# HGRN2 decay levels on 64 keys by 64 queries in place of 128 by 128

## The chip, the cores and the metric

The kernel runs on one core of one Trainium2 chip. The metric is device time in microseconds (us) of one execution; the median of several executions is compared. The profile is taken by the hardware profiler during one more execution of the same program, and all views of the trace below come from that one. Engines are named as the profile names them: PE is TensorE's matmul, PEld its weight load, DVE is VectorE, ACT is ScalarE, POOL is GpSimd, SP is SyncE.

## The reference

Two layers of a trunk over 640 tokens (512 latent tokens and 128 context tokens, width 1024). Each layer normalises and modulates its input, projects it once, mixes tokens in three ways (a Fourier transform, six heads of retention, six heads of HGRN2), projects back, and runs a SwiGLU feed-forward network. The part that the change touches is HGRN2, per head with 64 key and 64 value channels:

```python
rel = bc[:, :, :, None, :] - bc[:, :, None, :, :]
dec = jnp.exp(jnp.where(tri[:, :, None], rel, -jnp.inf))
A = jnp.sum(qc[:, :, :, None, :] * kc[:, :, None, :, :] * dec, axis=-1)
o = inter + jnp.einsum('bhij,bhjv->bhiv', A, vc)
```

Here bc is the running sum of the logarithm of the forget gate. Each pair of a query i and a key j is weighted, channel by channel, by the product of the gates between them. The scan runs once forward and once backward, and the two outputs are added. The reference uses chunks of 64 tokens; the kernel uses chunks of 128 and gets the same sums.

## The kernel before

**Stages.** A short start normalises the input and makes the first modulation. Then each layer has a stage of mixers (`mixers`, `hgrn`, `retention`, `fourier`) and a feed-forward stage (`feed`). The mixers of layer 0 lie between about 90 and 340 us of the trace, those of layer 1 between about 960 and 1170 us. Most of PE's time in both stages goes to products in which each operand is split into a high and a low part (lines 219 to 221, three products for one), whose weights ACT and DVE split on the fly (lines 206 and 207).

**HGRN2 by levels.** `hgrn(l, ct)` handles two heads at once: head 0 lies on partitions 0 to 63, head 1 on partitions 64 to 127. It runs four times in a layer: for ct = 0, 1 and 2 over the 512 latent tokens (nu = 4 chunks of 128) and once for the context tokens (nu = 3: its one chunk for each of the three pairs of heads). The scores of a chunk, transposed with keys on partitions and queries in columns, are built in AT. First a product without decay gives the diagonal (pd, line 809). Then seven levels follow, s = 1, 2, 4, ..., 64. At a level the chunk is cut into blocks of s tokens, and the two blocks of each neighbouring pair are queries and keys of each other. The product pl (line 824) is made over the whole chunk, all 128 keys by all 128 queries, though at level `lev` only the entries whose blocks are neighbours are wanted. For levels 0 to 4 these are picked by a copy under a mask (line 843, COPY_PREDICATED on DVE); for levels 5 and 6 ACT copies the wanted rectangles (line 847).

**Order within a level.** POOL multiplies the keys K by decays (line 832) and the table of decays Tm (line 835). ACT gathers the keys of the next level into C (line 799). DVE multiplies half of the queries Qx by decays (line 839); it can do so only when pl has read them, and the next pl waits for it. So the loop through PE is: pl of a level, Qx on DVE, pl of the next.

**Order of the work.** PE's order is written by the program: `Order` keeps a planned clock that `o.pe(us)` moves on, and generators such as `hgrn` give control back with `yield us` so that other units of work (projections of 2.6 or 3.9 us, parts of retention and of the Fourier transform) come in between. After each pl the clock is moved on by 0.44 * nu, and each level ends with `yield P["lev"]`, 2.4. The instructions of the other engines are put in order by a scheduler when the program is built. In layer 0 a further thread (`modulation`, lines 312 and 314) puts the remaining modulation on DVE, with loads from DRAM.

After the levels the keys are transposed (KT, line 867), states are built (U, line 697), and `cross_out` makes the output from S, Qx and AT (lines 737 and 741).

Of the kernel before, what the change touches and what calls it, by code (L numbers as in the profile page):

```python
# [11 lines left out]
U8 = mybir.dt.uint8  # L12
# [17 lines left out]
def pick(t2, p0, p1, off, dims):  # L30
    b = t2[p0:p1, 0:1]
    return bass.AP(b.tensor, b.offset + off, [list(list(b.ap)[0])] + [list(d) for d in dims])
# [119 lines left out]
class Kernel:  # L152
# [312 lines left out]
    def mixers(self, l, hT, mp):  # L465
        nc, a, o = self.nc, self.a, self.o
# [6 lines left out]
        self.raws, self.mix = [None] * 6, [None] * NK  # L473
        mskf = self.m4("mskf", (128, 7, 128))
        nc.sync.dma_start(mskf, a["masks"])
        self.msk = mp.tile([128, 7, 128], U8, name="msk")
        nc.vector.tensor_copy(self.msk, mskf)
        self.free(mskf)
        self.forget_bounds(l)
        self.PF, self.PK = self.m3("PF", (128, 2, 3, 128)), self.m3("PK", (128, 2, 3, 128))  # L480
# [285 lines left out]
    def hgrn(self, l, ct):  # L766

        nc = self.nc  # L770
        prev = {0: None, 1: 0, 2: 1, None: 2}[ct]
        need = [("B", 2 if ct is None else ct)] + ([("Hlast", prev)] if ct != 0 else [])
        yield lambda: self.have(*need) and self.can(m4=4, m2=3)
        self.mark(("H", ct))
        if ct is None:
            bases = (self.PF, self.PK, self.Pq)
            F, K = (t.rearrange("p d c w -> p d (c w)") for t in (self.PF, self.PK))
            q = self.Pq.rearrange("p c w -> p (c w)")
        else:
            bases = self.hg.pop(ct)  # L780
            F, K, q = bases
        nu = 3 if ct is None else 4
        W = nu * 128
        Qx = self.m4("Qx", (128, 2, W))
        ks = self.m2("ks", (128, W))
        nc.gpsimd.tensor_tensor(ks, K[:, 0, :], K[:, 1, :], ALU.add)
        nc.vector.tensor_tensor(Qx, F, q.unsqueeze(1).to_broadcast([128, 2, W]), ALU.mult)
        AT = self.m4("AT", (128, 2, nu, 128))
        Qf, Kf = Qx.rearrange("p d w -> p (d w)"), K.rearrange("p d w -> p (d w)")
        Tt, toff = F.rearrange("p d w -> p (d w)"), 0  # L790
        Tn, tnext = self.m4("Tm", (128, 2 * W)), 0

        Cs = deque(self.m2("C") for _ in range(2))

        def composite(lev):
            s = 1 << lev
            C = self.mem.again(Cs.popleft(), "C", (128, W))
            Cs.append(C)
            nc.scalar.copy(pick(C, 0, 128, 0, [[2 * s, W // s // 2], [s, 2], [1, s]]),
                           pick(Kf, 0, 128, 0, [[2 * s, W // s // 2], [W + s, 2], [1, s]]))  # L800
            return C

        C = composite(0)
        yield 2.0
        pd = [self.ps("pd") for _ in range(2)]
        for u in range(nu):
            for hh in range(2):
                pr, us = slice(64 * hh, 64 * hh + 64), slice(u * 128, (u + 1) * 128)
                nc.tensor.matmul(pd[hh][:, us], ks[pr, us], q[pr, us], start=True, stop=True)
        self.o.pe(0.44 * nu)  # L810
        self.free(ks, bases[2])
        for hh in range(2):
            nc.scalar.copy(AT[:, hh], pd[hh][:, 0:W].rearrange("p (u i) -> p u i", u=nu))
        yield 1.0
        S = None
        for lev in range(7):
            s = 1 << lev
            nb = W // s
            np_ = nb // 2
            pl = [self.ps("pl") for _ in range(2)]  # L820
            for u in range(nu):
                for hh in range(2):
                    p0 = 64 * hh
                    nc.tensor.matmul(pl[hh][:, u * 128:(u + 1) * 128], C[p0:p0 + 64, u * 128:(u + 1) * 128],  # L824
                                     pick(Qf, p0, p0 + 64, u * 128, [[2 * s, 64 // s], [W + s, 2], [1, s]]),
                                     start=True, stop=True)
            self.o.pe(0.44 * nu)

            for d in range(2):
                kv = pick(Kf, 0, 128, d * (W + s), [[2 * s, np_], [1, s]])  # L830
                tv = pick(Tt, 0, 128, toff + (nb + 1 if d == 0 else 0), [[2, np_], [0, s]])
                self.kv.tensor_tensor(kv, kv, tv, ALU.mult)
            if lev < 6:
                C = composite(lev + 1)
            self.kv.tensor_tensor(pick(Tn, 0, 128, tnext, [[np_, 2], [1, np_]]),
                                  pick(Tt, 0, 128, toff, [[nb, 2], [2, np_]]),
                                  pick(Tt, 0, 128, toff + 1, [[nb, 2], [2, np_]]), ALU.mult)
            qv = pick(Qf, 0, 128, 0, [[W + s, 2], [2 * s, np_], [1, s]])
            nc.vector.tensor_tensor(qv, qv, pick(Tt, 0, 128, toff + 1, [[nb - 1, 2], [2, np_], [0, s]]), ALU.mult)
            for hh in range(2):  # L840
                pv = pl[hh][:, 0:W].rearrange("p (u i) -> p u i", u=nu)
                if lev < 5:
                    nc.vector.copy_predicated(AT[:, hh], self.msk[:, lev, :].unsqueeze(1).to_broadcast([128, nu, 128]), pv)
                else:
                    for b in range(128 // s):
                        rows, cols = (slice(s * i, s * i + s) for i in (b, b ^ 1))
                        nc.scalar.copy(AT[rows, hh, :, cols], pv[rows, :, cols])
            Tt, toff, tnext = Tn, tnext, tnext + 2 * np_
            if lev == 0:
                self.free(bases[0])  # L850
            if lev == 5:
                self.free(*Cs)
            if lev == 4 and ct is not None:
                yield lambda: self.can(m4=1)
                S = self.new_states(l, 1, ct)
            if lev == 1:
                self.mark(("Hfree", ct))
            yield P["lev"]
        self.mark(("Hlast", ct))
        yield lambda: self.can(m3=1)  # L860
        pk = [self.ps("pk") for _ in range(2)]
        KT = self.m3("KT", (128, 2, 3, 128))
        for d in range(2):
            for n in range(3):
                u = n if ct is None or d == 0 else n + 1
                nc.tensor.transpose(pk[d][:, n * 128:(n + 1) * 128], K[:, d, u * 128:(u + 1) * 128], self.ident)
            nc.scalar.copy(KT[:, d], pk[d][:, 0:384].rearrange("p (n c) -> p n c", n=3))
        self.o.pe(0.7)
        self.free(bases[1])
        yield 1.6  # L870
        Tsc = lambda d, c: Tn[:, toff + (1 - d) * nu + c:toff + (1 - d) * nu + c + 1]
        yield lambda: self.have(*(("V", l, g, t) for g in (0, 1) for t in range(5)))
        self.cross_states(l, 1, ct, KT, Tsc, self.VH, S)
        self.free(Tn)
        yield P["co"]
        yield lambda: ct is None or self.can(ax=1)
        self.cross_out(1, ct, AT, S, (Qx[:, 1, :], Qx[:, 0, :]), self.VH)
        self.free(Qx)
        if ct is None:
            self.mark(("Hdone",), 0.0)  # L880
# [608 lines left out]
```

## Time and profile before

| what | value |
|---|---|
| median of 3 runs | 1744.54 us (1740.31 to 1745.72) |
| profiled execution | 1746.83 us |
| its span from first to last instruction | 1745.1 us |
| mean granted TensorE clock | 0.990 |
| busy: PE, DVE, ACT, POOL | 1683.2, 1072.5, 694.9, 451.5 us |

Busy times of different engines overlap. A busy time of PE is the union of its matmuls, each from its start to its modelled end; matmuls are pipelined and overlap, so how fast they follow one another is read from the starts and from the length of a run of equal ones. A product of float32 operands leaves two records for each call in the program, one of float32r operands leaves one.

### The profile page before, as it was taken

The numbers are of one execution on the slowest core, as the hardware profiler recorded it, in microseconds if no ns is written. First come the engines' busy times: TensorE is split into PE (matmuls) and PEld (weight loads), VectorE is DVE, ScalarE is ACT, GpSimd is POOL, SyncE is SP. The second block draws the span as 40 slices with busy tenths as digits, with TensorE's granted clock in tenths as the row PEclk, the third lists the DMA queues.
The fourth block names the chain that finished last, engine by engine and source line by source line (L and its number), as shares of the span: only waits on it lengthen the run. The fifth ranks groups of instructions, "written<-read, shape, count | busy, mean of one in ns | idle before, by whom it ended". The sixth has DMA issues, their size and how long they took to land.

```text
span 1745.1 us, 29155 instructions
## 1 busy us (share of the span) xinstructions
PE 1683.2 (96%) x11634; PEld 1547.1 (89%) x11634; DVE 1072.5 (61%) x1851; ACT 694.9 (40%) x1362; POOL 451.5 (26%) x473
## 2 busy tenths in 40 slices
PE   6989989999999999999999999999999999999997
PEld 4878878898999999989989998879799999999996
DVE  4597996548668776877484556674654434343428
ACT  4633443745544443434164444367253122121210
POOL 2233432103255453644052233220230000000001
PEclk9999989999999999999999999999999999999999
DMA  8544521242356554544222121113234222222301
GB/s 328 165 129 128 159 63 40 83 169 85 117 190 203 162 181 131 181 135 152 73 101 93 61 74 60 40 59 103 103 109 157 73 73 73 73 85 61 96 26 61
DMA packets 71239, 194.42 MB, mean 111 GB/s; under 512 B 12208, under 2 KB 12992, under 8 KB 71104
## 3 DMA queue, kind: packets, MB, share of 16 engines
q1 hardware_dynamic: 66816, 182.10, 32.5%
q0 software_dynamic: 4000, 10.35, 1.8%
q8 instruction: 91, 1.49, 0.3%
q14 instruction: 44, 0.36, 0.1%
q10 hardware_dynamic: 288, 0.11, 0.0%
HBM read 186.47 MB, written 6.06 MB: 110 GB/s over the span
## 4 chain that ended last, share of the span: by engine, by line
PE 80%; DVE 7%; ACT 3%; issue 2%; POOL 2%; DMA 1%; SPq 0%; DVEq 0%; ACTq 0%; POOLq 0%
PE pg L221 6%; PE pu L221 6%; PE pu L220 6%; PE pu L219 6%; PE pg L220 6%; PE pg L219 6%; PE dps L221 5%; PE dps L220 5%; PE dps L219 5%; PE pl L824 2%; PE p L219 2%; PE ops L221 2%; PE ops L219 2%; PE ops L220 2%; PE p L220 2%
## 5 line engine op out<-in xcount | busy, mean ns | idle before, releaser
L207 DVE TENSOR_TENSOR wlo<-wraw,whi 128x1024 fp32r<-128x1024 f32 x204 | 266.1, 1307 | 255.8 <-ACT whi L206 253.6
L206 ACT CAST whi<-wraw 128x1024 fp32r<-128x1024 f32 x206 | 215.1, 1048 | 405.9 <-PE pg L220 126.2
L316 POOL TENSOR_TENSOR wm<-wm,csb 128x512 f32<-128x512 f32 x112 | 179.8, 1625 | 183.0 <-DVE jb L312 156.8
L221 PE MATMUL pg<-h2T,wlo 128*128 128x384 f32 (+1 forms) x704 | 218.2, 310 | 3.0 <-DVE wlo L207 3.0
L219 PE MATMUL pg<-h2T,whi 128*128 128x384 f32 (+1 forms) x704 | 218.4, 310 | 0.0
L220 PE MATMUL pg<-h2T,whi 128*128 128x384 f32 (+1 forms) x704 | 217.8, 309 | 0.0
L220 PE MATMUL pu<-h2T,whi 128*128 128x384 f32 (+1 forms) x704 | 217.2, 308 | 0.0
L219 PE MATMUL pu<-h2T,whi 128*128 128x384 f32 (+1 forms) x704 | 217.2, 308 | 0.0
L221 PE MATMUL pu<-h2T,wlo 128*128 128x384 f32 (+1 forms) x704 | 217.2, 308 | 0.0
L340 POOL TENSOR_SCALAR bnve<-bnag 128x1 f32<-128x1 f32 x40 | 13.9, 351 | 645.9 <-DVE bnag L338 636.6
L219 PE MATMUL dps<-whi,ah 128*128 128x512 f32 x440 | 171.5, 390 | 0.0
L221 PE MATMUL dps<-whi,al 128*128 128x512 f32 x440 | 171.5, 390 | 0.0
L220 PE MATMUL dps<-wlo,ah 128*128 128x512 f32 x440 | 171.4, 389 | 0.0
L312 DVE SCALAR_TENSOR_TENSOR jb<-wm,csb 128x512 bf16<-128x512 f32 x160 | 149.0, 931 | 14.2 <-DMA wm<-in_w_modT 8.4
L221 PEld LDWEIGHTS pg<-h2T,wlo 128*128 128x128 f32 x704 | 134.0, 190 | 3.5 <-DVE wlo L207 3.4
L219 PEld LDWEIGHTS pg<-h2T,whi 128*128 128x128 f32 x704 | 134.2, 191 | 0.3
L220 PEld LDWEIGHTS pg<-h2T,whi 128*128 128x128 f32 x704 | 134.2, 191 | 0.3
L289 ACT ACTIVATE wm<-wm 128x512 f32<-128x512 f32 x112 | 70.8, 632 | 158.1 <-POOL wm L316 157.8
L221 PEld LDWEIGHTS pu<-h2T,wlo 128*128 128x128 f32 x704 | 133.6, 190 | 0.0
L220 PEld LDWEIGHTS pu<-h2T,whi 128*128 128x128 f32 x704 | 133.6, 190 | 0.0
L219 PEld LDWEIGHTS pu<-h2T,whi 128*128 128x128 f32 x704 | 133.6, 190 | 0.0
L1194 DVE TENSOR_TENSOR sg<-sg,pu 128x256 f32<-128x256 f32 x88 | 42.7, 485 | 119.8 <-PE pu L221 112.9
(273 smaller groups left out, 3830.5 us busy)
## 6 DMA issues: line engine op xcount, KB each, us to landing
wm<-in_w_modT SPq DMA_DIRECT2D x160, 256.0 KB, 2.9
wraw<-in_w_gate SPq DMA_DIRECT2D x44, 512.0 KB, 3.7
wraw<-in_w_up SPq DMA_DIRECT2D x44, 512.0 KB, 3.6
wraw<-in_w_down SPq DMA_DIRECT2D x44, 512.0 KB, 3.6
wraw<-in_w_fm SPq DMA_DIRECT2D x42, 512.0 KB, 3.6
wm<-in_w_mod SPq DMA_DIRECT2D x16, 512.0 KB, 10.2
wraw<-in_w_tm SPq DMA_DIRECT2D x16, 512.0 KB, 3.5
wraw<-in_w_out SPq DMA_DIRECT2D x16, 512.0 KB, 3.7
```

What stands on the lines that cost most here:

```text
L206: self.nc.scalar.copy(hi, raw)
L207: (eng or self.nc.vector).tensor_tensor(lo, raw, hi.bitcast(F32), ALU.subtract)
L219: mm(out, lh, rh, start=first, stop=False)
L220: mm(out, lh, rl, start=False, stop=False)
L221: mm(out, ll, rh, start=False, stop=last)
L289: keep(nc.scalar.activation(out=t, in_=t, func=AF.Copy, accum_out=d))
L312: keep(nc.vector.scalar_tensor_tensor(self.jb, wt, 1.0, csb[0], ALU.mult, ALU.mult, accum_out=d[0]))
L316: nc.gpsimd.tensor_tensor(wt, wt, csb[1], ALU.mult)
L340: nc.gpsimd.tensor_scalar(ve, ag[:, 1:2], EPS, None, ALU.add)
L824: nc.tensor.matmul(pl[hh][:, u * 128:(u + 1) * 128], C[p0:p0 + 64, u * 128:(u + 1) * 128], pick(Qf, p0, p0 + 64, u * 128, [[2 * s, 64 // s ...
L1194: nc.vector.tensor_tensor(sg, sg, pu[:, :n], ALU.mult)
```

## The change

The level products are made for halves of a chunk. Keys 0 to 63 meet only queries 0 to 63, and keys 64 to 127 only queries 64 to 127; each such product has 64 channels, 64 keys and 64 queries, and takes one quarter of the array: the head gives the rows, the half of the keys gives the columns. Up to level 5 the wanted pairs lie inside a half. At level 6 (s = 64) each half's keys meet the other half's queries. So there are 16 calls for nu = 4 where there were 8, in the order head 0 with half 0, head 0 with half 1, head 1 with half 0, head 1 with half 1, and then the next chunk.

Results are gathered in 64 columns: pd and pl fill half a bank of PSUM, and while levels 0 to 5 run, AT holds its scores in columns 0 to 63 of each chunk. Copies from pd and the masked copies are over half as many columns, and the mask has 5 levels and 64 columns in place of 7 and 128. At level 6 one more ACT copy moves the scores of the keys 64 to 127 to columns 64 to 127; then the two copies for each head fill the off-diagonal quarters. What is charged to the planned clock and the yields are as before.

```diff
-        self.msk = mp.tile([128, 7, 128], U8, name="msk")
-        nc.vector.tensor_copy(self.msk, mskf)
+        self.msk = mp.tile([128, 5, 64], U8, name="msk")
+        for b in (slice(0, 64), slice(64, 128)):
+            nc.vector.tensor_copy(self.msk[b], mskf[b, 0:5, b])
...
-        pd = [self.ps("pd") for _ in range(2)]
-        for u in range(nu):
-            for hh in range(2):
-                pr, us = slice(64 * hh, 64 * hh + 64), slice(u * 128, (u + 1) * 128)
-                nc.tensor.matmul(pd[hh][:, us], ks[pr, us], q[pr, us], start=True, stop=True)
+        A = AT.rearrange("p h u i -> p (h u) i")
+
+        def halves(name):
+            return [self.ps(name)[:, 0:W // 2].rearrange("p (u i) -> p u i", u=nu) for _ in range(2)]
+
+        def blocks():
+            for u in range(nu):
+                for hh in range(2):
+                    for b in range(2):
+                        t0 = u * 128 + 64 * b
+                        yield slice(64 * hh, 64 * hh + 64), slice(64 * b, 64 * b + 64), hh, u, b, t0
+
+        pd = halves("pd")
+        for pr, rows, hh, u, b, t0 in blocks():
+            nc.tensor.matmul(pd[hh][rows, u], ks[pr, t0:t0 + 64], q[pr, t0:t0 + 64], start=True, stop=True)
         self.o.pe(0.44 * nu)
         self.free(ks, bases[2])
         for hh in range(2):
-            nc.scalar.copy(AT[:, hh], pd[hh][:, 0:W].rearrange("p (u i) -> p u i", u=nu))
+            nc.scalar.copy(AT[:, hh, :, 0:64], pd[hh])
...
-            pl = [self.ps("pl") for _ in range(2)]
-            for u in range(nu):
-                for hh in range(2):
-                    p0 = 64 * hh
-                    nc.tensor.matmul(pl[hh][:, u * 128:(u + 1) * 128], C[p0:p0 + 64, u * 128:(u + 1) * 128],
-                                     pick(Qf, p0, p0 + 64, u * 128, [[2 * s, 64 // s], [W + s, 2], [1, s]]),
-                                     start=True, stop=True)
+            pl = halves("pl")
+            for pr, rows, hh, u, b, t0 in blocks():
+                if lev < 6:
+                    qs = pick(Qf, pr.start, pr.stop, t0, [[2 * s, 32 // s], [W + s, 2], [1, s]])
+                else:
+                    qs = Qf[pr, (1 - b) * W + t0 + 64 - 128 * b:(1 - b) * W + t0 + 128 - 128 * b]
+                nc.tensor.matmul(pl[hh][rows, u], C[pr, t0:t0 + 64], qs, start=True, stop=True)
...
+            if lev == 6:
+                nc.scalar.copy(A[64:128, :, 64:128], A[64:128, :, 0:64])
             for hh in range(2):
-                pv = pl[hh][:, 0:W].rearrange("p (u i) -> p u i", u=nu)
                 if lev < 5:
-                    nc.vector.copy_predicated(AT[:, hh], self.msk[:, lev, :].unsqueeze(1).to_broadcast([128, nu, 128]), pv)
+                    nc.vector.copy_predicated(AT[:, hh, :, 0:64], self.msk[:, lev, :].unsqueeze(1).to_broadcast([128, nu, 64]),
+                                              pl[hh])
+                elif lev == 5:
+                    for b in range(4):
+                        rows, cols = slice(32 * b, 32 * b + 32), slice(32 - 32 * (b % 2), 64 - 32 * (b % 2))
+                        nc.scalar.copy(AT[rows, hh, :, cols], pl[hh][rows, :, cols])
                 else:
-                    for b in range(128 // s):
-                        rows, cols = (slice(s * i, s * i + s) for i in (b, b ^ 1))
-                        nc.scalar.copy(AT[rows, hh, :, cols], pv[rows, :, cols])
+                    for b in range(2):
+                        rows = slice(64 * b, 64 * b + 64)
+                        nc.scalar.copy(AT[rows, hh, :, 64 - 64 * b:128 - 64 * b], pl[hh][rows])
```

## Rows read from the trace of the kernel before

**Rows 1.** The page: busy us by engine, share of the span, instructions.
```profile
PE 1683.2 (96%) x11634; PEld 1547.1 (89%) x11634; DVE 1072.5 (61%) x1851; ACT 694.9 (40%) x1362; POOL 451.5 (26%) x473
```

**Rows 2.** The page: the chain that ended last, share of the span by engine.
```profile
PE 80%; DVE 7%; ACT 3%; issue 2%; POOL 2%; DMA 1%; SPq 0%; DVEq 0%; ACTq 0%; POOLq 0%
```

**Rows 3.** Windows of the mixers: busy us (records) by engine, clock, DMA share, GB/s.
```profile
90.00:270.00 180.00, 159.31 (x1363) 144.00 (x1364) 158.99 (x336) 69.97 (x164) 64.05 (x76) 0.95 0.39 118
960.00:1170.00 210.00, 206.36 (x1941) 183.74 (x1940) 128.18 (x235) 94.66 (x223) 69.15 (x92) 0.99 0.20 61
```

**Rows 4.** What PE waited for, 90 to 340 us: total, times, longest.
```profile
PE pl L824 <- DVE Qx L839: 17.9, 12, 3.5
PE pr L906 <- DVE rx L542: 3.7, 2, 2.7
```

**Rows 5.** What PE waited for, 960 to 1170 us.
```profile
PE pr L906 <- DVE rx L542: 2.1, 2, 1.8
PE pl L824 <- ACT K L512: 0.7, 1, 0.7
```

**Rows 6.** Instructions of lines 824 and 809: duration ns min/median/max, first and last start.
```profile
L824 PE MATMUL pl<-Qx,C x840: 272/272/580, 97.1 to 1155.7; 64*128 64x128 f32 x168
...
L809 PE MATMUL pd<-q,ks x96: 272/272/373, 92.9 to 1070.0; 64*128 64x128 f32 x96
```

**Rows 7.** PE by time: pl of level 2, and its first records alone (start, length).
```profile
107.88 1.16 PE L824 MATMUL pl<-Qx,C 64*128 64x128 f32 x16 [0.20 <-DVE Qx L839]
...
107.88 0.60 PE L824 MATMUL pl<-Qx,C 64*128 64x128 f32 x6 [0.20 <-DVE Qx L839]
```

**Rows 8.** PE by time: pl of level 2 for nu = 3.
```profile
279.70 0.94 PE L824 MATMUL pl<-Qx,C 64*128 64x128 f32 x12
```

**Rows 9.** PE by time: pl of level 0 and of level 1.
```profile
97.07 1.57 PE L824 MATMUL pl<-Qx,C 64*128 64x128 f32 x16
...
103.39 1.23 PE L824 MATMUL pl<-Qx,C 64*128 64x128 f32 x16 [1.68 <-DVE Qx L839]
```

**Rows 10.** PE by time: U, products with 64 columns, whole and first records alone.
```profile
144.59 0.92 PE L697 MATMUL U<-VH,KT 128*64 128x64 f32 x24
...
144.59 0.63 PE L697 MATMUL U<-VH,KT 128*64 128x64 f32 x14
```

**Rows 11.** PE by time: the first modulation, four products side by side.
```profile
46.85 0.64 PE L248 MATMUL modps<-wm,cs 128*32 128x128 f32 x16
...
49.19 0.86 PE L248 MATMUL modps<-wm,cs 128*32 128x128 f32 x24
```

**Rows 12.** Groups by line and form: busy us, mean ns, idle before.
```profile
L843 DVE COPY_PREDICATED AT<-msk,pl 128x512 f32<-128x512 uint8 x60 | 42.5, 730 | 9.8 <-PE pl L824 9.8
...
L799 ACT COPY C<-K 128x512 f32<-128x512 f32 x42 | 28.0, 666 | 35.8 <-POOL K L832 16.7 <-PE pl L824 14.1 <-PE fp L220 4.2
...
L843 DVE COPY_PREDICATED AT<-msk,pl 128x384 f32<-128x384 uint8 x20 | 11.2, 582 | 5.0 <-PE pl L824 5.0
...
L813 ACT COPY AT<-pd 128x512 f32<-128x512 f32 x12 | 6.4, 590 | 3.5 <-PE pd L809 3.5
```

**Rows 13.** All engines by time, layer 1: from pl of level 0 to the next.
```profile
965.44 1.57 PE L824 MATMUL pl<-Qx,C 64*128 64x128 f32 x16
967.12 0.75 DVE L843 COPY_PREDICATED AT<-msk,pl 128x512 f32<-128x512 uint8 x1 [5.94 <-PE pl L824]
...
967.76 0.68 DVE L839 TENSOR_TENSOR Qx<-Qx,F 128x512 f32<-128x512 f32 x1
...
970.01 1.25 PE L824 MATMUL pl<-Qx,C 64*128 64x128 f32 x16
```

**Rows 14.** The chain that ended last, layer 0, 97 to 130 us: start, length, what.
```profile
98.54 2.99 DMA wm<-in_w_modT
...
102.13 0.63 DVE AT L843
102.77 0.57 DVE Qx L839
```

## The prediction

> **What bounds the kernel now.** I read the page first: PE is busy for 96% of the span and DVE for 61% [rows 1], and the chain that ended last runs through PE for 80% and through DVE for 7% [rows 2]. So time taken from PE shortens the run, wherever PE would not wait instead. The windows of the two mixer stages show where that is in doubt [rows 3]. In layer 1 PE is busy for 206.4 of 210 us. In layer 0 PE idles for 20.7 of 180 us, while DVE is busy for 159.0. The waits of PE say for whom: in layer 0 pl waits for Qx on DVE, 17.9 us in 12 places [rows 4]; in layer 1 it waits 0.7 us once, for another engine, and never for Qx [rows 5]. So layer 1 is bound by PE, and layer 0 in turn by PE and by a DVE that is full. In the chain of layer 0 a masked copy stands directly ahead of the Qx for which PE waits [rows 14].
>
> **How fast small products follow one another.** The line's own view gives 840 records of pl, 120 a level, that is two records for a call, and 96 of pd at nu = 4 [rows 6]. A pl of level 2 for nu = 4 has 8 calls, 16 records, and lasts 1.16 us; its first 6 records last 0.60 [rows 7]. The 10 others take 0.56 us: five rounds of 0.112 us, and in each round both heads make one pass, on their own 64 rows of the array. Two tiles thus run side by side. At nu = 3 the group lasts 0.94 us [rows 8]. U has tiles of 64 columns and streams 64 columns: 24 records last 0.92 us, the first 14 of them 0.63 [rows 10], so a round of two tiles takes 0.29/5 = 0.058 us. Half the streamed columns cost half the time, and tiles beside each other in columns also run together, each on a stream of its own. The first modulation has four tiles of 32 columns: 24 records take 0.22 us more than 16 [rows 11], two rounds of four in 0.11 us each, as long as the two-tile round of pl with as many streamed columns. No row shows two halves of the rows and two halves of the columns at work at once. Both kinds of neighbours are shown, though, and so are four streams.
>
> **Removed and added on PE.** The new group has 16 calls, 32 records, on four tiles. If all four run together it has 8 rounds of 64 columns, where U has 12. From U: 0.92 - 4 x 0.058 = 0.69 us, and 0.01 for starting two more tiles: 0.70 in place of 1.16, so 0.46 us less. At nu = 3 there are 6 rounds: 0.92 - 6 x 0.058 + 0.01 = 0.58 in place of 0.94, so 0.36 less. Over both layers there are 6 groups of pd and 30 of levels 2 to 6 at nu = 4: 36 x 0.46 = 16.6 us. At nu = 3 there are 12: 4.3 us. Sum 20.9.
>
> Levels 0 and 1 are slower now, 1.57 and 1.23 us [rows 9]; they stream single elements and pairs from places far apart. In the new group two streams read the same partitions. If together they are no faster than the one stream now, these levels gain nothing. If each keeps the rate of the old stream, the part above 1.16 halves: level 0 takes 0.70 + 0.20 = 0.90 and gains 0.67, level 1 takes 0.74 and gains 0.49; at nu = 3 three quarters of that. That is 6 x 1.16 + 2 x 0.87 = 8.7 us. No row tells which; I take the middle, 4.4. PE saves 25.3 us in all (20.9 to 29.6), 12.6 in each layer.
>
> One rule speaks against this. U shows 0.058 us for a round of 64 streamed columns, and pl 0.112 for 128 [rows 7, 10]: a fixed cost of 0.004 us at most. The Trainium skill, TensorEngine Tiling (Array Packing), section Performance Considerations, puts about 60 cycles of overhead on each matmul on TRN2 and advises against tiling along a dimension that is already small. At 2.4 GHz that would be an estimated 0.025 us on each round, 0.2 us for each group of eight, and with it PE would save some 25.3 - 12 = 13 us by that page; by the rows it saves 25.3.
>
> **DVE.** A masked copy takes 0.730 us at 512 columns and 0.582 at 384 [rows 12]: 0.148 for 128. The same slope gives 0.434 at 256 and 0.36 at 192. The bounds are half of 0.730 and the whole 0.582, the row at 384. 60 x 0.296 + 20 x 0.222 = 22.2 us of DVE time go, 11.1 in each layer; by the bounds 11 to 28 in all. In layer 1 DVE is not the bound, so this is worth nothing there by itself. In layer 0, where DVE is full, a level loses two copies, 0.59 us, which is more than the 0.46 that PE loses.
>
> **ACT.** Copies from pd shrink from 512 to 256 columns. The bounds are nothing and half of 0.590 [rows 12]; I take 0.2 us each, 16 copies, 3 us less. Level 6 gets a copy of 64 x 512, eight in all. Its nearest rows are copies of 512 columns, 0.590 and 0.666 [rows 12]: 5 us more. On ACT's queue it stands behind the copies of level 5, and what is queued behind it are four copies of level 6, the copies of the transposed keys, for which U waits, and the splits of weights. ACT is busy for 70 of 180 and 95 of 210 us [rows 3], so I cost it at nothing; with that cover gone it is 8 x 0.6 = 5 us. The copies of levels 5 and 6 keep their shapes. The mask's conversion is two short DVE instructions in place of one, twice in the run: nothing. No DMA is added or moved, and the planned clock is charged as before, so PE's units keep their order. The scheduler may order the other engines a little differently, which I can't price.
>
> **What reaches the end.** Layer 1: the loop runs from the end of pl to Qx on DVE and to the next pl. After level 0 pl's run ends at 967.0, Qx at 968.4, and the next pl starts at 970.0, because other work of PE lies between [rows 13]. That work stays, so the loop has its 1.6 us of slack still, and 0.3 more because the masked copy ahead of Qx is shorter. POOL is busy for 69 of 210 us [rows 3]. So all 12.6 us count. Layer 0: where DVE is the bound, a level shortens by up to 0.59 us, where PE is, by 0.46. Some of DVE's idle time there is a load of weights, 2.99 us once [rows 14], and that does not shorten. I take 10.5 of the 12.6, with 5.5 as the lower bound (masked copies at 0.582: 30 x 0.148 + 10 x 0.1) and 14 as the upper. The sum is 12.6 + 10.5 = 23 us. The profiled execution took 1746.8 us, which gives 1724; it lies 2.3 us above the median 1744.5, so against that I predict 1721.5.
>
> **The rivals.** *A, as worked out:* four tiles together. With the bounds, layer 1 gives 10.5 to 14.8 and layer 0 5.5 to 14: 16 to 29 us less, 1716 to 1729.
>
> *B, half of it:* the tiles overlap, but something shared stretches the rounds: two scattered streams at every short s, a fixed cost by round, or layer 0 held by DVE's other work. For it: levels 0 and 1 are slower already [rows 9]. Against it: U's rounds of 0.058 [rows 10]. Half of A, 8 to 16 us less: 1729 to 1737. By the page's overhead the run would end here too.
>
> *C, only two at a time:* then 16 rounds of 0.058 last as long as 8 of 0.112, and PE saves nothing. Against it: the four streams of the modulation [rows 11]. What stays is DVE's 11.1 us in layer 0, of which the 17.9 us of waits [rows 4] may give back 3 to 8: 1737 to 1742, about half of it beyond what can be told from no change. A difference under 0.3%, 5.2 us, is no difference here.
>
> *D, slower:* neighbours in rows and columns exclude one another, so that 32 passes run singly: 31 x 0.058 + 0.3 = 2.1 us for a group, 0.94 more than now, at nu = 3 24 passes, 1.6, 0.7 more: 48 x 0.94 + 16 x 0.7 = 56 us, about 1800. It decides from the point where a group is 0.08 us longer than now (64 x 0.08 = 5.2). For it: no row has a tile with neighbours of both kinds. Against it: either kind alone costs nothing [rows 7, 10].
>
> **How the numbers follow.** A 0.70, B 0.13, C 0.09, D 0.08. The range 1714 to 1738 takes in A's bounds with 2 us for the scheduler's order, and B; C and D stay out. Faster by over 0.3% are A, B and half of C: 0.87. Within it is the other half of C: 0.05. Slower is D: 0.08.
>
> **What would show it.** Line 824's successor with twice the records, in forms of 64 x 64; a group of level 2 of 32 records in 0.70 us, of level 0 in 0.9 to 1.6 (its place between tells of the shared stream); masked copies of 256 columns at 0.43 us; no wait of pl for Qx in layer 1; in layer 0 waits for Qx of no more than 18 us; both mixer stages shorter by 10 to 13 us, and the feed-forward stages as long as before. The prediction is wrong if the group stays near 1.16 us or above, or if pl's gain comes back as PE waiting for Qx, for C, or for the copies of the transposed keys behind the new ACT copy.

## The result, and the profile after

The changed kernel takes 1720.20 us, the median of 4 runs (1717.92 to 1721.84). Beside it the kernel before took 1742.58 (4 runs, 1740.31 to 1745.72). The ratio is 0.9858, with a 95% interval of 0.984 to 0.9876: faster by 22.4 us, where 1721.5 was forecast. The profiled execution took 1721.84, of which 1719.8 are the span; it is the one that the rows below show. Against the profiled execution before, the span is 25.3 us shorter.

First the page of the kernel after: busy us by engine, and the chain that ended last.

```profile
PE 1656.2 (96%) x12594; PEld 1523.6 (89%) x12594; DVE 1055.8 (61%) x1853; ACT 695.8 (40%) x1370; POOL 455.5 (26%) x473
...
PE 78%; DVE 8%; ACT 3%; issue 3%; POOL 2%; DMA 2%; SPq 0%; DVEq 0%; POOLq 0%; ACTq 0%
```

The picture of [rows 1, 2] is the same one, with 27.0 us less of PE and 16.7 less of DVE. PE by time, pl of level 0, level 1 and level 2 at nu = 4, then of the same levels at nu = 3 (start, length):

```profile
97.13 0.90 PE L839 MATMUL pl<-Qx,C 64*64 64x64 f32 x32
...
103.97 0.72 PE L839 MATMUL pl<-Qx,C 64*64 64x64 f32 x32 [2.87 <-DVE Qx L852]
...
109.17 0.69 PE L839 MATMUL pl<-Qx,C 64*64 64x64 f32 x32
...
258.49 0.72 PE L839 MATMUL pl<-Qx,C 64*64 64x64 f32 x24
...
262.21 0.61 PE L839 MATMUL pl<-Qx,C 64*64 64x64 f32 x24
...
266.41 0.58 PE L839 MATMUL pl<-Qx,C 64*64 64x64 f32 x24
```

These answer to [rows 7 to 9]. Twice the records, and level 2 goes from 1.16 to 0.69 us; at nu = 3 from 0.94 to 0.58. Level 0 goes from 1.57 to 0.90 and level 1 from 1.23 to 0.72. At nu = 3 the trace of before has 1.25 and 0.99 for these two:

```profile
270.71 1.25 PE L824 MATMUL pl<-Qx,C 64*128 64x128 f32 x12
274.96 0.99 PE L824 MATMUL pl<-Qx,C 64*128 64x128 f32 x12
```

Over the run that is 36 x 0.47 + 12 x 0.36 + 6 x (0.67 + 0.51) + 2 x (0.53 + 0.38) = 16.9 + 4.3 + 7.1 + 1.8 = 30.1 us of PE, 15.0 in each layer. The groups of the vector engine, of the copies on ACT, and of the two kinds of product (busy us, mean ns, idle before):

```profile
L839 PE MATMUL pl<-Qx,C 64*64 64x64 f32 x1680 | 40.4, 234 | 17.4 <-DVE Qx L852 16.6 <-ACT K L513 0.8
...
L857 DVE COPY_PREDICATED AT<-msk,pl 128x256 f32<-128x256 uint8 x60 | 25.5, 441 | 7.6 <-PE pl L839 7.6
...
L857 DVE COPY_PREDICATED AT<-msk,pl 128x192 f32<-128x192 uint8 x20 | 6.9, 367 | 5.2 <-PE pl L839 5.2
L822 PE MATMUL pd<-q,ks 64*64 64x64 f32 x192 | 4.4, 225 | 0.0
```

The masked copies take 441 and 367 ns where the slope of [rows 12] had given 434 and 360. They fall from 42.5 + 11.2 to 25.5 + 6.9, 21.3 us less of DVE.

Where the 25 us came from is read from the stages. Each window runs from the first pd of a layer to its first pgt, the product that ends the mixers; between the two lies the rest of layer 0 (busy us and records of PE, PEld, DVE, ACT, POOL, then the granted clock). Before:

```profile
92.90:324.50 231.60, 209.54 (x1888) 185.96 (x1888) 191.00 (x404) 97.41 (x224) 76.80 (x92) 0.96 0.33 102
...
324.50:961.30 636.80, 629.76 (x3864) 591.19 (x3862) 433.20 (x711) 289.32 (x576) 247.61 (x205) 0.99 0.44 139
...
961.30:1169.10 207.80, 204.16 (x1925) 181.75 (x1924) 127.01 (x233) 93.57 (x220) 69.15 (x92) 0.99 0.19 59
```

After:

```profile
93.20:311.90 218.70, 197.56 (x2369) 175.92 (x2368) 182.89 (x406) 98.22 (x228) 80.80 (x92) 0.94 0.34 109
...
311.90:947.00 635.10, 628.19 (x3862) 589.65 (x3860) 434.43 (x712) 288.71 (x576) 247.63 (x205) 1.00 0.43 140
...
947.00:1143.90 196.90, 190.90 (x2404) 169.96 (x2404) 117.37 (x233) 94.23 (x224) 69.30 (x92) 0.98 0.20 63
```

Layer 0's mixers are 12.9 us shorter, layer 1's 10.9, and the stretch between 1.7, at a clock of 1.00 in place of 0.99. That 1.7 is not the change's: in e7 below, the change with one more copy, the stretch takes 636.6. The window from layer 1's pgt to the end differs by less than 0.2. In layer 1 PE's busy time falls by 13.3 and its idle time grows from 3.6 to 6.0. In layer 0 it falls by 12.0, 3 less than the groups gave back, while the granted clock goes from 0.96 to 0.94; PE's idle time stays, 22.1 and 21.1. Each view is of one execution, and e7 shows how far two differ: there the two mixer stages take 216.3 and 195.5 us, where the change has 218.7 and 196.9. Who PE waits for there, first in layer 0 and then in layer 1 (total, times, longest):

```profile
PE pl L839 <- DVE Qx L852: 14.3, 8, 3.8
PE pr L925 <- DVE rx L543: 5.0, 2, 3.0
PE pl L839 <- ACT K L513: 0.8, 1, 0.8
...
PE pr L925 <- DVE rx L543: 2.9, 2, 1.9
PE pl L839 <- DVE Qx L852: 2.3, 4, 1.2
```

Against [rows 4, 5], the wait for Qx in layer 0 is 3.6 us smaller. In layer 1, where it was nothing, it is now 2.3.

### The profile page after: what moved, and what is told of

It is laid out like the page before. It is cut to its first block, busy times and chain, and to the rows that moved or that the text cites. A ratio compares the mean times of both kernels' runs of the same rounds, so it can differ in the third digit from the quotient of the medians.

```text
span 1719.8 us, 31088 instructions
## 1 busy us (share of the span) xinstructions
PE 1656.2 (96%) x12594; PEld 1523.6 (89%) x12594; DVE 1055.8 (61%) x1853; ACT 695.8 (40%) x1370; POOL 455.5 (26%) x473
## 4 chain that ended last, share of the span: by engine, by line
PE 78%; DVE 8%; ACT 3%; issue 3%; POOL 2%; DMA 2%; SPq 0%; DVEq 0%; POOLq 0%; ACTq 0%
PE pg L221 6%; PE pu L219 6%; PE pu L221 6%; PE pu L220 6%; PE pg L220 6%; PE pg L219 6%; PE dps L221 6%; PE dps L220 6%; PE dps L219 6%; PE ops L221 2%; PE ops L219 2%; PE ops L220 2%; PE pgt L219 2%; PE pgt L221 2%; PE pgt L220 2%
```

## The experiments

Two theories about the time stood at the start. By theory 1, layer 1 gains by PE's shorter groups and layer 0 by DVE's shorter masked copies, since DVE is what is full there. By theory 2, all of it is PE's. (The quoted expectations number theories of their own, each anew.) The kernels have labels, e1 to e12. Each is the changed one with one edit, if nothing else is said; its time stands beside the kernel before, run along with it on the same chip (1743.29 us beside e1 to e4, 1744.19 beside e5 to e8, 1743.34 beside e9 to e12).

**Two tiles at a time (e1).** The same calls in another order, so that neighbours in the queue use both halves of the rows and one half of the columns:

```diff
-            for u in range(nu):
-                for hh in range(2):
-                    for b in range(2):
+            for b in range(2):
+                for u in range(nu):
+                    for hh in range(2):
```

> The changed kernel with one thing undone: the calls of a group run over all chunks with half 0 first and then with half 1, so only the two heads' tiles can work side by side; work, shapes and copies are those of the changed kernel. Theory 1 (the gain is PE's, from four tiles at once): a group of level 2 lasts 16 x 0.058 + 0.23 = 1.16 us again, PE gets back 24 to 30 us, and the run takes 1738 to 1746 us, 20 to 25 more than the changed kernel; the shorter masked copies alone are worth 0 to 5 us. Theory 2 (the gain is DVE's, from shorter masked copies): the run stays at 1718 to 1724 us, and PE waits less for Qx as its groups get longer.

1728.65 us (1728.28 to 1728.91), ratio 0.9921 (0.9905 to 0.9936). Slower than the change, and far from what two tiles were to cost.

**One tile at a time (e3).** The loop order is hh, b, u, so that four calls follow one another on one tile.

> The changed kernel with the calls of a group in an order that fills one tile after another: head 0 half 0 over all chunks, then head 0 half 1, and so on. Theory 1 (tiles overlap only where calls that follow one another use different tiles): 32 passes of 0.058 us one by one, a group of level 2 lasts 31 x 0.058 + 0.3 = 2.1 us instead of 0.70, 84 us more on PE, and the run takes 1785 to 1805 us, slower than the kernel before. If PE reorders matmuls of free tiles: 0.70 us and no change, 1718 to 1724. Theory 2 (PE's groups don't matter): 1718 to 1730.

1741.64 us in its one run, beside 1743.29. PE by time, pl of level 2, first with two tiles, then with one:

```profile
106.29 0.98 PE L839 MATMUL pl<-Qx,C 64*64 64x64 f32 x32
```

```profile
107.49 1.54 PE L839 MATMUL pl<-Qx,C 64*64 64x64 f32 x32
```

So how many calls stand side by side is what sets the group's length: 0.69, 0.98 and 1.54 us for the same 32 records. In rounds of 0.058 us, the two-tile group is 5 longer than the eight of the change, 13 and not 16; the one-tile group is 15 longer, 23 and not 32. When one tile's calls change to the next tile's, about three rounds overlap. The starts of the records in these two groups show it: in three rounds at each change two records start together in e3, where otherwise one does, and four in e1, where otherwise two do. That is one reason why both expectations were too long. The other is that the time does not follow the groups: over the run pl and pd are busy 16 us more in e1 and 48 in e3, about half of it in each layer, and the kernels are 8.5 and 21.4 us slower. The windows of layer 0's mixers and of layer 1's say where. First e1's:

```profile
92.20:311.30 219.10, 202.37 (x2368) 181.20 (x2368) 181.58 (x404) 98.46 (x228) 80.21 (x92) 0.96 0.33 108
948.40:1150.60 202.20, 197.53 (x2404) 176.86 (x2404) 117.88 (x233) 94.45 (x224) 68.31 (x92) 0.99 0.19 61
```

Then e3's:

```profile
93.10:314.40 221.30, 214.41 (x2367) 193.73 (x2367) 182.34 (x404) 98.91 (x227) 78.28 (x92) 0.98 0.33 107
949.60:1163.80 214.20, 212.23 (x2405) 191.90 (x2404) 117.98 (x233) 95.37 (x224) 66.82 (x92) 1.00 0.18 58
```

Layer 1 is 5.3 us longer than with the change in e1 and 17.3 in e3. Layer 0 is only 0.4 and 2.6 longer: in e3 PE is busy there for 16.9 us more but idle for 6.9 us in place of 21.1. There PE's longer groups mostly fill time in which it would have waited for Qx, and the clock is 0.98 in place of 0.94.

**DVE's price put back (e2).** A second masked copy of nu - 2 chunks behind each one, which writes the same values again:

```diff
                                               pl[hh])
+                    nc.vector.copy_predicated(AT[:, hh, 0:nu - 2, 0:64],
+                                              self.msk[:, lev, :].unsqueeze(1).to_broadcast([128, nu - 2, 64]),
+                                              pl[hh][:, 0:nu - 2])
```

> The changed kernel with DVE's saving undone: behind each masked copy a second one repeats it for nu - 2 chunks, 0.29 us more at nu = 4 and 0.22 at nu = 3, so that a level costs DVE about what it did before, 0.73 and 0.58 us for each head. Theory 1 (PE's gain): layer 1 stays as it is, layer 0 gets 2 to 8 us longer because DVE is full there; 1722 to 1729 us. Theory 2 (DVE's gain): the run goes back to 1738 to 1744 us, in both layers alike.

1719.54 us (1716.12 to 1721.83), ratio 0.9873 (0.9853 to 0.9893). The groups of masked copies show that DVE really got the work, 16.6 us of it in the 60 larger copies alone:

```profile
L857 DVE COPY_PREDICATED AT<-msk,pl 128x256 f32<-128x256 uint8 x60 | 25.3, 440 | 7.0 <-PE pl L839 7.0
L859 DVE COPY_PREDICATED AT<-msk,pl 128x128 f32<-128x128 uint8 x60 | 16.6, 295 | 0.2
```

The time is that of the change: nearly all of what DVE had saved was put back, and nothing was lost. So what theory 1 says of layer 0 has nothing for it, with one reservation: the scheduler also put 30 of DVE's some 420 other instructions up to the first pgt in other places (those outside the longest sequence that both kernels have in common), and a loss made good by that order is not excluded.

**PE's price put back (e5).** Every call of pd and pl is made twice, the second into a half of the bank that nobody reads:

```diff
+            for g in range(2):
-            for pr, rows, hh, u, b, t0 in blocks():
+                for pr, rows, hh, u, b, t0 in blocks():
...
-                nc.tensor.matmul(pl[hh][rows, u], C[pr, t0:t0 + 64], qs, start=True, stop=True)
+                    nc.tensor.matmul(pl[hh][rows, g, u], C[pr, t0:t0 + 64], qs, start=True, stop=True)
```

> The changed kernel with every call of pd and pl made twice, the second time into an unused half of the bank, all four tiles at once: only DVE's and ACT's part of the change is left, since a group of level 2 has 16 rounds of 0.058 us and lasts 0.70 + 8 x 0.058 = 1.17 us, as before the change. Theory 1 (the gain is PE's): PE gets back all 30 us of its groups, and the run takes 1738 to 1744 us, within 0.3% of the kernel before; in layer 0 some of it may come out of waits and of time at the lower clock. Theory 2 (a good part is DVE's): 1725 to 1735 us.

1740.03 us (10 runs, 1735.25 to 1742.31), ratio 0.9973 (0.9962 to 0.9984). A group of level 2 is back at the length it had before:

```profile
108.24 1.16 PE L842 MATMUL pl<-Qx,C 64*64 64x64 f32 x64
```

Of the 22.4 us some 20 are gone, with DVE's copies still short. By the total, theory 2 stands. By the stages it does not: layer 1 is 8.4 us longer than with the change, and layer 0 is 10.7 longer, where longer groups cost e1 and e3 next to nothing. The windows of e5, layer 0 and layer 1:

```profile
91.30:320.70 229.40, 209.12 (x3329) 187.97 (x3328) 180.63 (x406) 98.51 (x228) 77.93 (x92) 0.96 0.34 105
957.40:1162.70 205.30, 202.44 (x3365) 181.88 (x3364) 116.28 (x233) 94.79 (x224) 67.85 (x92) 1.00 0.21 61
```

Layer 0 takes 229.4 us here and 221.3 with one tile at a time (e3), where PE had 5.3 us *more* to do; the difference is idle time, 20.3 against 6.9. So something other than PE's sum decides in layer 0. The records of DVE between pl of level 2 and of level 3 show one place. With the calls twice:

```profile
109.29 1.22 DVE L207 TENSOR_TENSOR wlo<-wraw,whi 128x1024 fp32r<-128x1024 f32 x1
...
111.48 1.65 DVE L207 TENSOR_TENSOR wlo<-wraw,whi 128x1024 fp32r<-128x1024 f32 x1
...
113.65 0.68 DVE L856 TENSOR_TENSOR Qx<-Qx,Tm 128x512 f32<-128x512 f32 x1
114.48 0.70 PE L842 MATMUL pl<-Qx,C 64*64 64x64 f32 x33 [2.02 <-DVE Qx L856]
```

With one tile at a time:

```profile
110.26 1.11 DVE L852 TENSOR_TENSOR Qx<-Qx,Tm 128x512 f32<-128x512 f32 x1
...
112.03 1.19 PE L839 MATMUL pl<-Qx,C 64*64 64x64 f32 x25
```

Two splits of weights stand ahead of Qx on DVE in the one, none in the other. From the end of pl to the next pl it takes 5.1 us against 3.0; in the kernel before it is 4.9 (a split of 1.64 us ahead), in the changed one 3.8 (one split of 1.22). One place does not decide, though: e1 takes 5.1 us here, with a split of 1.64 ahead of Qx, and its layer 0 is as short as the change's. Over all of layer 0, the order of PE's calls is the same in these kernels but for pd and pl themselves. DVE's is not: of its some 420 instructions up to the first pgt, counted in the same way, none stands elsewhere than in the change in e7, 5 in e1, 19 in e3, 31 in the kernel before and 53 in e5. Theory 3: the scheduler, which presumably reckons with the new groups' sizes and not with whether they run side by side, puts the work of the other engines, Qx on DVE among it, in another order, and this order is the part of layer 0's gain that PE's sum does not explain.

**Qx with priority (e4, e9, e10).** One line asks the scheduler to put Qx first, in the changed kernel (e4), then in the kernel before (e9), then with the calls twice (e10):

```diff
-            nc.vector.tensor_tensor(qv, qv, pick(Tt, 0, 128, toff + 1, [[nb - 1, 2], [2, np_], [0, s]]), ALU.mult)
+            with self.tc.high_priority(offset=2000):
+                nc.vector.tensor_tensor(qv, qv, pick(Tt, 0, 128, toff + 1, [[nb - 1, 2], [2, np_], [0, s]]), ALU.mult)
```

> The changed kernel with a high priority on DVE's product Qx, so that it stands ahead of both masked copies of its level where the scheduler had put one of them first. If PE's waits in layer 0 (14.3 us for Qx) are partly for that masked copy of 0.44 us: 8 to 12 waits get 0.4 us shorter, and stretches at the lower clock that follow them may go; 1712 to 1718 us. Rival: the waits are for the modulation's products on DVE (0.69 us each, two to four in a row), which keep their place: 1718 to 1723 us and waits as long as now.

1717.58 us (1717.49 to 1719.14), ratio 0.9859 (0.9843 to 0.9876): no difference from the change that can be told. PE's waits for Qx fall from 16.6 us to 10.1 over the run, and those for rx grow from 7.9 to 12.1.

> The kernel before, with nothing of the change, in which only Qx gets priority in the scheduler, so that on DVE it goes ahead of the splits of weights and the products of the modulation where they were put before it. PE's order stays that of the kernel before. Theory 1, what is left of layer 0's gain beside PE's shorter groups is the order of DVE: layer 0's mixers then get some 4 to 6 us shorter here too, the time is 1737 to 1740, ratio 0.996 to 0.998, and the first pgt starts near 319 in place of 324.5. Theory 2, the gain is the change's own, shorter groups and shorter masked copies: 1742 to 1746, ratio 0.999 to 1.001, first pgt at 324 to 325.

1748.97 us (1747.34 to 1752.86), ratio 1.0035 (1.0021 to 1.0049): not shorter but 5.6 us longer. The records show that the edit did not do what it was for. Between level 2 and level 3 a split still stands ahead of Qx:

```profile
111.44 1.22 DVE L207 TENSOR_TENSOR wlo<-wraw,whi 128x1024 fp32r<-128x1024 f32 x1
...
113.64 1.11 DVE L840 TENSOR_TENSOR Qx<-Qx,Tm 128x512 f32<-128x512 f32 x1
```

> The changed kernel with every call of pd and pl made twice, as in the run that made them twice at 1740.03 us, and Qx with priority. The second calls write to a half of the bank that nobody reads. Theory 1, that run lost some 4 to 6 us to the order of DVE in layer 0 beside PE's longer groups: 1733 to 1736 here, ratio 0.993 to 0.995, first pgt near 315. Theory 2, it lost them to PE alone: 1739 to 1742 again, ratio 0.997, first pgt at 320 to 321.

1737.45 us (1736.88 to 1738.21), ratio 0.9964 (0.9951 to 0.9977): not told apart from 1740.03, and here too both splits are ahead of Qx (109.39 and 111.58, Qx at 113.14). Both expectations of theory 3 were missed, and since neither kernel got the order that it asks for, e9 and e10 settle nothing. e1, e3 and e5 say more. In e1 DVE's order is nearly the change's and ACT's is the same; PE's groups are 8 us longer in layer 0, and the stage takes as long, 219.1 us against 218.7. In e3 and e5 DVE, ACT and POOL do the same work, and e3's groups are the longer ones; still its layer 0 is 8.1 us shorter, more than the 2.4 between the change and e7. What is left between these two is the number of calls and the order (57 of DVE's instructions, 7 of ACT's and 7 of SP's stand elsewhere). So by elimination the order makes several us in layer 0. No run changes the order alone, e3 ran once, and which instructions it hangs on is not shown.

**The new copy on ACT, twice (e7).** The copy of 64 x 512 at level 6 is made a second time.

> The changed kernel with the new ACT copy of level 6 made twice (eight more copies of 64 x 512, about 0.6 us each). If ACT has room there, as was assumed when it was costed at nothing: 1718 to 1722 us, no change. If the copies of the transposed keys and the splits behind it are on the path: up to 5 us more, 1725.

1719.32 us (1716.59 to 1721.46), ratio 0.9857 (0.9841 to 0.9874). It costs nothing, and its double costs nothing.

**Less modulation in layer 0's mixers (e6, e8), and more (e11).** DVE does the products of the modulation between the levels, at a pace set in the planned clock. `pace0` goes from 2.8 to 3.4 (e6), to 4.0 (e8), and, with Qx's priority, to 2.4 (e11).

> The changed kernel with the modulation of layer 0 spread out: its planned distance between two pieces is 3.4 in place of 2.8, the work is the same. If the waits of pl for Qx (14.3 us in layer 0) come from a DVE that is full of modulation, they fall to 3 to 8 us, and the time at the lower clock in the mixers of layer 0, 27 us in seven stretches, falls to 17 or less: 1705 to 1714 us. Rival: the waits come from the level's own chain, and the modulation only fills gaps: 1717 to 1722 us. If the modulation comes too late for the gates of layer 0, the stage after it waits: over 1722.

1732.82 us (1731.31 to 1737.64), ratio 0.994 (0.9921 to 0.996).

> As the run with the planned distance 3.4, but 4.0. The same reasons: waits for Qx in layer 0 at 0 to 5 us, 1702 to 1712 us, unless the modulation's end (about 310 us into the run by the planned clock's pace) meets retention's work on DVE, which PE waits for at line 925 now for 5 us: then it gains less than 3.4, 1710 to 1718 us. Rival as there: no change.

1738.24 us (1736.47 to 1739.89), ratio 0.9964 (0.9951 to 0.9977). PE's waits over the whole of it:

```profile
PE pl L839 <- DVE Qx L852: 11.4, 11, 2.1
PE pr L925 <- DVE rx L543: 10.5, 5, 5.1
PE pl L839 <- ACT C L800: 7.8, 4, 2.7
...
PE pl L839 <- DVE jb L314: 4.2, 1, 4.2
```

The wait for Qx falls from 16.6 to 11.4, and others take its place: for rx, for C, for the modulation itself. And some of the mixers' work on PE now comes behind the first pgt: layer 0's mixers take 221.2 us up to there, and the stretch from there to layer 1 takes 651.2 in place of 635.1.

> The changed kernel with Qx's priority and the modulation of layer 0 paced at 2.4 in place of 2.8 units of the planned clock. Slower paces made the kernel slower (3.4: 1732.8, 4.0: 1738.2), since the work came later and PE waited for it in the stage behind. If that is the whole of it, a faster pace gives back some of it: 1712 to 1716, ratio 0.982 to 0.984. The rival: at 2.4 DVE's products of the modulation stand ahead of the levels' Qx and PE waits for that, 1720 to 1728, ratio 0.986 to 0.991.

1717.07 us (1713.71 to 1717.97), ratio 0.9845 (0.983 to 0.9861): neither expectation, the same as at 2.8. Of the four paces 2.4 and 2.8 are not told apart, and the two slower ones lose; moving work out of layer 0 is no remedy.

**Another charge in the plan (e12).** With Qx's priority, `self.o.pe(0.44 * nu)` behind pd and pl becomes `0.2 * nu`.

> The changed kernel with Qx's priority, and a planned clock that is charged 0.2 in place of 0.44 for each chunk of a group of pd or pl, as the shorter groups take. The other work that the plan puts between the levels then comes later by the plan's clock or in another place. If the old charge no longer fits the shorter groups, the order gets better and the time is 1710 to 1715, ratio 0.980 to 0.983. The rival, that the order of units was tuned at the old charge and any other is worse: 1720 to 1730, ratio 0.986 to 0.992.

1751.50 us (1749.78 to 1752.66), ratio 1.0048 (1.0032 to 1.0065). This is 34 us above the kernel with Qx's priority alone (e4), more than the whole gain. The levels of layer 0 now end earlier, and work that used to lie between them comes behind: it takes 43.5 us from the transposes of HGRN2's last keys to pgt, in place of 17.8. Against e4, layer 0's mixers are 4.8 us longer, the stretch behind them 16.2 and layer 1's mixers 9.2. So the charge is not a duration that one corrects: it holds the order of the units in place.

No version beats the changed kernel by more than the intervals tell.

## Why the prediction was right, and where it was not

*PE's groups.* Four tiles run together: 0.70 and 0.58 us were worked out from U, and 0.69 and 0.58 measured (the 0.01 in it for starting two more tiles, for which no row stood, is not seen). Rival A's mechanism is what happened, and the order of the calls (0.98 and 1.54 us in e1 and e3) shows that it is the tiles side by side that do it. The term of 20.9 us measured 21.2.

*Levels 0 and 1.* The term was 4.4, the middle of 0 to 8.7; it measured 8.9. Two scattered streams that read the same partitions each keep the rate of the one stream before, so the upper bound was the truth. PE's saving was 30.1 and not 25.3 us.

*The page's overhead.* By the Trainium skill, TensorEngine Tiling (Array Packing), Performance Considerations, a matmul on TRN2 carries about 60 cycles of overhead. Read as an addition to each round, as the prediction read it, the trace does not agree: a round of 64 columns stays at 0.058 us, one of 128 takes 0.112, and PE saved 30 us, not 13. The 13 was no fair sum either: it put the overhead on top of rounds that the row of U had measured whole, with any overhead in them.

*Layer 1.* 12.6 us were to arrive, on the reason that the loop over Qx had slack to spare. That PE's groups make the gain here is shown: with groups of 0.69, 0.98, 1.16 and 1.54 us the stage takes 196.9, 202.2, 205.3 and 214.2 us (the change, e1, e5, e3). The groups gave 15.0 and the stage 10.9. PE's idle time grew by 2.4, most of it waits for Qx that were to stay at nothing; the rest went with the clock, 0.98 after 0.99. The slack was there at level 0 [rows 13], where it was looked at, and not at every level.

*Layer 0.* 10.5 were predicted and 12.9 came, but the step behind it failed. DVE was taken for the bound and a level was to shorten by the 0.59 us of its two masked copies. With that work put back the time stayed at 1719.5 (e2). PE's own saving does not carry it either: with groups 8 us longer than the change's, layer 0 took 219.1 us (e1), and with groups longer than before 221.3 (e3), 10.3 less than the kernel before. What remains is the order of the other engines: "The scheduler may order the other engines a little differently", which the prediction left without a price in the sum and gave 2 us in the range. How much of the 12.9 it makes stays open. In e5, with groups of 1.16 us again, DVE got neither the change's order nor the old one (40 of its instructions stand elsewhere than in the kernel before), so the 10.7 us that were lost in its layer 0 are not a measure of PE's groups.

*ACT and the rest.* The copy on ACT at nothing was right (e7). The feed-forward stages kept their length, as forecast.

*The sum.* The forecast was 25.3 us saved on PE and 23 at the end; it was 30.1 and, from span to span, 25.3. The errors cancel in part: more was saved than thought, more of it was lost in waits and at a lower clock, and layer 0's half came by an order that had no price in the sum. That the total came so close is in part luck. The medians differ by 22.4, since the profiled execution of before lay 4.2 us above its median here (1746.8 and 1742.58) and that of after 1.6.

*Rivals C and D.* They did not happen, but e1 and e3 are their cases, built by hand, and their prices were too high. C's 16 rounds are 13, D's 2.1 us for a group is 1.54. By e3, D's end would have been about 1742 here, and not 1800: more than half of PE's extra time went into waits that were there anyway.

## What to carry to other kernels

Small products on a quarter of the array pay when neighbours in the queue are on different tiles: with the same 32 records, the order of the calls made 0.69, 0.98 or 1.54 us of a group. Where two engines take turns, as in layer 0 here, neither engine's saved time can be added up into the end: put each one's work back by itself and see what is lost. And a shorter instruction also changes what a scheduler puts around it, so compare the order on the other engines before a gain is put down to the instruction.

## What the runs showed of the hardware that was not expected

The calls of one tile overlap with those of the next one in the queue by about three rounds of 0.058 us (13 and 23 rounds in place of 16 and 32, and records that start together in three rounds at each change), so tiles that seem to run in turn do so only in part.

Where PE's work got shorter and its waits stayed, its clock fell. Layer 0 ran at a mean granted clock of 0.96 before the change, 0.94 after it, and 0.98 with one tile at a time, where PE idled least; of the 15.0 us that the groups gave back there, its busy time fell by 12.0. Over whole executions the clock was 0.986 to 0.991 in the changed kernel's four and 0.989 to 0.993 in those of the kernel before. One such stretch of the kernel after, in windows (length, then busy us and records of PE, PEld, DVE, ACT, POOL, then the clock):

```profile
205.00:210.00 5.00, 3.94 (x79) 2.90 (x78) 4.93 (x12) 3.65 (x10) 4.54 (x6) 1.00 0.54 175
210.00:213.00 3.00, 1.04 (x32) 0.85 (x32) 3.00 (x8) 1.24 (x3) 2.67 (x3) 0.61 0.49 149
213.00:216.00 3.00, 2.02 (x36) 1.93 (x37) 3.00 (x9) 2.39 (x7) 1.97 (x2) 0.50 0.31 95
216.00:219.00 3.00, 3.00 (x22) 3.00 (x20) 3.00 (x7) 0.03 (x1) 1.67 (x2) 0.75 0.41 136
```

PE waits for Qx behind a DVE that is busy throughout, works for 1.04 of 3 us, and then goes on at half clock, 1.2 GHz of 2.4, well after its work is back: pl of level 2 took 1.13 us at 213.98, in place of 0.69.
